# A one-core encoder step: mask products over 128 rows, and the last down set, final norm and output in an order written out by hand

## The chip, the cores and the metric

The kernel runs on one core of a Trainium2 chip. The metric is the device time of one execution in microseconds (us). Below, the engines have short names: PE is TensorE (matrix products; PEld its weight loads), DVE is VectorE, ACT is ScalarE, POOL is GpSimd, and SP is the engine that issues most transfers.

## What is computed

One layer of a streaming encoder, for 1024 prompt frames and 64 sample frames (1088 columns), with 1024 features. Two places matter here.

```python
s = einsum("bqhd,bkhd->bhqk", q, k) * SOFTMAX_SCALE
visible = (k_pos // CHUNK) <= (q_pos // CHUNK)        # CHUNK = 64 frames
s = where(visible, s, -1e30); p = softmax(s)
...
h = h + square(relu(rmsnorm(h, g_mlp) @ w_up)) @ w_down   # 1024 -> 4096 -> 1024
y = rmsnorm(h, g_final)       # h * rsqrt(mean(h*h) + 1e-6) * g_final
```

## The kernel before

**Attention.** For each of 8 heads and each of 8 blocks `i` of 128 queries, `scores` forms a score tile `S` in PSUM from three products (lines L1180 to L1182: every operand is split into a high and a low part), over 96 rows for even heads and 128 rows for odd ones. Only the last 128 columns of a tile need a mask, and it is added by one more product, L1184: `lhsT=mrow[:, 0:128], rhs=mrow[:, 128:256]`. `mrow` has one row: 128 zeros and ones, and 128 values that are 0 or -1e30; the product of the two halves is a 128x128 block that is -1e30 where a key isn't visible. There are 64 of these products. `negm` (DVE) takes the row maximum, ACT the exponential, PE transposes the result (`tr`, L1198), and PE multiplies with the values (`po`, L1208 to L1211). Up to three score tiles are in flight ahead of their transposes.

**The last down set.** The MLP's products are done by a scheme with 7 products in place of 8 on 2x2 blocks (`SEQ = "XYXYXZX"` names the PSUM tile of each of the 7; `TAKE` says which quarter `q[k][t]` of the output each is added to). A *set* `(g, jp)` is 7 products: `g` is one of 8 slices of the hidden features, `jp` one of two halves of the output features. The 1088 columns are two blocks `t` of 544 (`NH`), each in two halves `c` of 272 (`NC`). The last set (`g == 7, jp == 1`) does all 7 products for `c = 0`, then for `c = 1`, so that the final norm of the first columns can start early. Product `i` for one `c` is 12 matmuls of 272 columns (two feature blocks `jl`, two `k`, three high/low combinations), and is then added into `q` on DVE (`dn_evac`, L1809).

**Final norm and output.** `final_first` squares and sums the features that are final before the last set; `final_half(c, t)` squares the others on ACT, sums them (on PE, `col_sum`, into 68x4 columns), takes 1/sqrt by `rsqrt_col` (DVE, one ACT square root, DVE), spreads the result over 128 partitions by four transposes on PE (L1876), and multiplies: for `t = 1` ACT applies the gain and POOL the rows (L1885), for `t = 0` DVE does both in one instruction (L333), one bank of PSUM being read. 16 transfers of 272 KB write `y`, 14 issued by SP and 2 by ACT. All of this is written as generators that a `pump()` advances after each product, and a scheduler places each engine's instructions.

Of the kernel before, what the change touches and what calls it, by code (L numbers as in the profile page):

```python
# [22 lines left out]
EPS = 1e-6  # L23
# [6 lines left out]
def tile_hybrid_step(ctx: ExitStack, tc: tile.TileContext, I: dict, O: dict):  # L30
# [828 lines left out]
    mrow = phq.tile([1, 256], F32R, name="mrow")  # L859
    mraw = raw1([1, 256], "mraw")  # L860
# [953 lines left out]
    sqp, fin = [], []  # L1814

    def final_first():

        for c in range(2):
            cc = slice(NC * c, NC * c + NC)
            sqp.append(rq([128, 2, NC], f"fsq{c}"))  # L1820
            for t in range(2):
                s_ = rq([128, 2, 2, NC], f"fp{c}{t}")
                for k in range(2):
                    act.activation(s_[:, k], q4[k][t][:, 0:2, cc], AF.Square)
                e = dve if t else pool
                e.tensor_tensor(s_[:, 0], s_[:, 0], s_[:, 1], op=ALU.add)
                e.tensor_tensor(sqp[c][:, t], s_[:, 0, 0], s_[:, 0, 1], op=ALU.add)
                yield
        for k in range(2):
            for j in range(2):  # L1830
                z = q4[k][1][:, j]
                act.activation(z, z, AF.Copy, scale=g_fi[:, 4 * k + j:4 * k + j + 1])
            yield

    def final_half(c, t):

        cc = slice(NC * c, NC * c + NC)
        end = c == 1 and t == 0
        pr_ = fin[c][:, t]
        ps = pr_[:, NC:512]  # L1840
        sq = [wr4([128, 2, NC], f"fs{c}{t}{k}") for k in range(2)]
        ks = (0, 1)

        def col_sum(z, n):
            for j in range(4):
                pe.matmul(ps[:TT, 4 * n + j:4 * n + j + 1], lhsT=z[:, TT * j:TT * j + TT], rhs=ones, start=True, stop=True)

        if end:
            col_sum(sqp[c][:, t], 0)
        for k in ks:  # L1850
            for j in range(2):
                act.activation(sq[k][:, j], q4[k][t][:, 2 + j, cc], AF.Square)
                if end:
                    col_sum(sq[k][:, j], 1 + 2 * k + j)
            yield
        cl_ = [x[:TT, 4 * t:4 * t + 4] for x in col[:3]]
        tot = ps[:TT, 0:4]
        if end:
            tot = col[3][:TT, 0:4]
            dve.tensor_reduce(tot, ps[:TT, 0:20].rearrange("p (n j) -> p j n", j=4), axis=mybir.AxisListType.X, op=ALU.add)  # L1860
        else:
            e = dve if t else pool
            e.tensor_tensor(sq[0], sq[0], sq[1], op=ALU.add)
            e.tensor_tensor(sq[0][:, 0], sq[0][:, 0], sq[0][:, 1], op=ALU.add)
            e.tensor_tensor(sq[0][:, 0], sq[0][:, 0], sqp[c][:, t], op=ALU.add)
            yield
            col_sum(sq[0][:, 0], 0)
        rsqrt_col(cl_[0], tot, 1024, cl_[1:])
        if t:
            for k in range(2):  # L1870
                for j in range(2):
                    z = q4[k][t][:, 2 + j, cc]
                    act.activation(z, z, AF.Copy, scale=g_fi[:, 4 * k + 2 + j:4 * k + 3 + j])
        yield
        for j in range(4):
            pe.transpose(pr_[:, TT * j:TT * j + TT], cl_[0][:, j:j + 1].to_broadcast([TT, 128]), ident[:TT, :TT])  # L1876
        c0 = NH * t + NC * c
        if t:
            rows = rq([128, NC], f"f{c}{t}w")
            act.copy(rows, pr_[:, :NC])  # L1880
# [12 lines left out]
    for g in range(8):  # L1893
        for jp in range(2):
            last = g == 7 and jp == 1
            made = {}
            for cs in ([[0], [1]] if last else [[0, 1]]):
# [3 lines left out]
                for i, x in enumerate(SEQ):  # L1901
# [3 lines left out]
                    for jl in range(2):  # L1905
# [4 lines left out]
                        if last:  # L1910
                            o = o[:, jl:jl + 1]
# [138 lines left out]
```

## Time and profile before

| what | value |
|---|---|
| median of 3 runs | 1413.93 us (1413.08 to 1417.74) |
| the profiled execution's own time | 1413.71 us |
| its span, first to last instruction | 1411.6 us |
| mean granted TensorE clock, as a share of full speed | 0.973 |
| busy: PE / PEld / DVE / ACT / POOL | 94% / 90% / 75% / 47% / 48% of the span |

The profile is of one execution. The 2.1 us between its span and its own time lie outside of the instructions. PE is busy nearly throughout, so what counts is where PE's time goes, and what is left at the end when PE has no products any more.

### The profile page before, as it was taken

Reading aid. Unit: us, or ns where it says so; the run is one execution under the profiler, and the core shown is the slowest. Engines: PE = TensorE matmul, PEld = TensorE weight load, DVE = VectorE, ACT = ScalarE, POOL = GpSimd, SP = SyncE. Lnnn points to the kernel's source line nnn. Section 1 sums busy time; section 2 is a strip of 40 time slices with the busy share of each in tenths; the row PEclk is TensorE's granted clock in tenths of the full one; section 3 lists DMA queues with packets and bytes.
Section 4 is the critical chain, followed back from the end, with each engine's and each line's share of the span. In section 5 each row is a group of like instructions: output and inputs, shape, how many; then the busy total and the mean of one; then the engine's idle time right before and its main releaser. Section 6 shows DMA issues by size and latency. Waiting matters only on the chain.

```text
span 1411.6 us, 24894 instructions
## 1 busy us (share of the span) xinstructions
PE 1321.5 (94%) x9544; PEld 1264.7 (90%) x9544; DVE 1055.7 (75%) x1675; ACT 667.1 (47%) x1335; POOL 680.6 (48%) x642
## 2 busy tenths in 40 slices
PE   6999999989999996999789999999989999999994
PEld 6999988977887786999789999999979999999994
DVE  7679789775888767557895566565699788888766
ACT  6476577665777753223342332332446433334332
POOL 3656756151435426252465455455547446454543
PEclk9999999999999998999899999999999999999996
DMA  5111101210333234022224443443568345563103
GB/s 215 62 41 41 44 28 47 74 34 8 59 59 73 68 114 132 1 92 75 85 84 146 162 157 114 157 156 118 200 238 291 123 156 170 175 187 110 60 1 127
DMA packets 81145, 151.24 MB, mean 107 GB/s; under 512 B 10114, under 2 KB 28675, under 8 KB 81027
## 3 DMA queue, kind: packets, MB, share of 16 engines
q1 hardware_dynamic: 80482, 149.10, 32.9%
q8 instruction: 75, 1.23, 0.3%
q10 hardware_dynamic: 544, 0.56, 0.1%
q14 instruction: 44, 0.35, 0.1%
HBM read 98.53 MB, written 41.40 MB: 99 GB/s over the span
## 4 chain that ended last, share of the span: by engine, by line
PE 70%; DVE 14%; issue 4%; ACT 4%; DMA 3%; POOL 3%; SPq 0%; DVEq 0%; ACTq 0%; POOLq 0%
PE X L1653 3%; PE X L1654 3%; PE X L1652 3%; PE dX L1652 3%; PE dX L1654 3%; PE dX L1653 3%; PE pw L1473 2%; PE pw L1475 2%; PE tr L1198 2%; PE pw L1474 2%; POOL wl L51 2%; PE dY L1654 2%; DVE ho L51 2%; PE dY L1652 2%; PE Y L1652 2%
## 5 line engine op out<-in xcount | busy, mean ns | idle before, releaser
L51 POOL TENSOR_TENSOR wl<-ws,wl 128x512 fp32r<-128x512 f32 x101 | 161.1, 1596 | 235.6 <-ACT wl L1546 228.6
L51 POOL TENSOR_TENSOR wl<-wr,wl 128x512 fp32r<-128x512 f32 x135 | 209.7, 1562 | 106.3 <-ACT wl L1546 100.8
L1546 ACT CAST wl<-ws 128x512 fp32r<-128x512 f32 x102 | 63.4, 622 | 196.7 <-DVE ws L1534 95.5
L1652 PE MATMUL dX<-to,wl 128*128 128x272 f32 x496 | 144.0, 290 | 2.9 <-DVE q L1809 2.0
L1653 PE MATMUL dX<-to,wl 128*128 128x272 f32 x496 | 142.9, 288 | 0.7 <-DVE to L51 0.7
L1654 PE MATMUL dX<-to,wl 128*128 128x272 f32 x496 | 143.4, 290 | 0.0
L1652 PE MATMUL X<-ho,wl 128*128 128x272 f32 x448 | 128.0, 290 | 5.4 <-DVE rb L1671 3.8
L1653 PE MATMUL X<-ho,wl 128*128 128x272 f32 x448 | 128.8, 288 | 0.5 <-DVE ho L51 0.5
L1654 PE MATMUL X<-ho,wl 128*128 128x272 f32 x448 | 128.9, 289 | 0.0
L1546 ACT CAST wl<-wr 128x512 fp32r<-128x512 f32 x136 | 83.9, 621 | 89.3 <-PE dX L1654 34.7
L1809 DVE TENSOR_TENSOR q<-dX,q 128x544 f32<-128x544 f32 (+1 forms) x116 | 79.4, 697 | 29.1 <-PE dX L1654 28.9
L1532 DVE TENSOR_TENSOR ws<-wr,wr 128x512 f32<-128x512 f32 x34 | 28.1, 826 | 93.9 <-DMA wr<-in_w_up_dram 74.8
L1652 PEld LDWEIGHTS dX<-to,wl 128*128 128x128 f32 x496 | 93.4, 188 | 4.2 <-DVE q L1809 1.6
L1653 PEld LDWEIGHTS dX<-to,wl 128*128 128x128 f32 x496 | 94.0, 190 | 1.0 <-DVE to L51 1.0
L1654 PEld LDWEIGHTS dX<-to,wl 128*128 128x128 f32 x496 | 93.3, 188 | 0.0
L1652 PEld LDWEIGHTS X<-ho,wl 128*128 128x128 f32 x448 | 83.6, 188 | 6.7 <-DVE rb L1671 4.2
L1653 PEld LDWEIGHTS X<-ho,wl 128*128 128x128 f32 x448 | 84.4, 188 | 0.7 <-DVE ho L51 0.7
L51 DVE TENSOR_TENSOR to<-rr,to 128x1088 fp32r<-128x1088 f32 x56 | 84.1, 1506 | 1.0 <-ACT to L1727 1.0
L1654 PEld LDWEIGHTS X<-ho,wl 128*128 128x128 f32 x448 | 84.2, 188 | 0.0
L1652 PE MATMUL dY<-to,wl 128*128 128x272 f32 x256 | 74.5, 291 | 2.8 <-DVE rb L333 1.8
L1654 PE MATMUL dY<-to,wl 128*128 128x272 f32 x256 | 75.0, 293 | 1.6 <-POOL wl L51 1.6
L1653 PE MATMUL dY<-to,wl 128*128 128x272 f32 x256 | 74.0, 289 | 0.0
(685 smaller groups left out, 4706.5 us busy)
## 6 DMA issues: line engine op xcount, KB each, us to landing
rr<-rd SPq DMA_DIRECT2D x56, 544.0 KB, 5.0
wr<-in_w_up_dram SPq DMA_DIRECT2D x36, 512.0 KB, 4.4
wr<-in_w_dn_dram SPq DMA_DIRECT2D x32, 512.0 KB, 4.7
rd<-rc SPq DMA_DIRECT2D x16, 544.0 KB, 3.6
rd<-re SPq DMA_DIRECT2D x16, 544.0 KB, 3.5
rd<-ra SPq DMA_DIRECT2D x28, 272.0 KB, 2.6
xw<-in_x_dram SPq DMA_DIRECT2D x8, 544.0 KB, 7.3
hp<-in_x_dram SPq DMA_DIRECT2D x4, 1088.0 KB, 13.2
```

The lines of the kernel that those rows point to most:

```text
L51: eng.tensor_tensor(out, src, hi, op=ALU.subtract)
L1198: pe.transpose(tr[:, 128 * j:128 * j + 128], Pt[:, 128 * (j0 + j):128 * (j0 + j) + 128], ident)
L1473: pe.matmul(o, lhsT=w[kt][0][:, m_], rhs=rh, start=(kt == 0), stop=False)
L1474: pe.matmul(o, lhsT=w[kt][0][:, m_], rhs=rl, start=False, stop=False)
L1475: pe.matmul(o, lhsT=w[kt][1][:, m_], rhs=rh, start=False, stop=(kt == 3))
L1532: dve.tensor_tensor(s_, a21, a22, op=ALU.add)
L1546: act.copy(w[:, 0], src)
L1652: pe.matmul(o, lhsT=lh, rhs=rh, start=first, stop=False, skip_group_check=True)
L1653: pe.matmul(o, lhsT=lh, rhs=rl, start=False, stop=False, skip_group_check=True)
L1654: pe.matmul(o, lhsT=ll, rhs=rh, start=False, stop=last, skip_group_check=True)
L1809: dve.tensor_tensor(z, o[:, :, :NC], z, op=ALU.add)
```

## The change

`mrow` becomes 128 rows, the first as before and 127 of zeros, in the kernel and in the constant that is loaded. The mask product therefore runs over 128 rows; its result is the same.

The last set, the final norm and the output are taken out of the loop and of the generators and are written out in one list under `tc.manual_schedule()`, in which each engine keeps the order of the list. The small chain of the norm works on PSUM (`v`) where it worked on SBUF. For the last columns (`c = 1`) the rows are transposed twice, into the tile `dY` (`ps`) for DVE and into the tile `fin` for an ACT copy that POOL reads, so that both engines multiply. All early sums of squares go to POOL.

```diff
-    mrow = phq.tile([1, 256], F32R, name="mrow")
-    mraw = raw1([1, 256], "mraw")
+    mrow = phq.tile([128, 256], F32R, name="mrow")
+    mraw = raw1([128, 256], "mraw")
...
+    def norm_f(ps, t):
+
+        v, o = ps[:TT, t, NC:NC + 4], col[t][:TT, 0:4]
+        dve.tensor_scalar(v, v, 1.0 / 1024, EPS, op0=ALU.mult, op1=ALU.add)
+        act.activation(o, v, AF.Sqrt)
+        yield
+        dve.reciprocal(o, o)
+        dve.tensor_tensor(v, v, o, op=ALU.mult)
+        stt(v, v, -0.5, o, ALU.mult, ALU.mult)
+        stt(o, v, 1.5, o, ALU.add, ALU.mult)
+
+    def rows_f(ps, t):
+
+        for j in range(4):
+            pe.transpose(ps[:, t, TT * j:TT * j + TT], col[t][:TT, j:j + 1].to_broadcast([TT, 128]), ident[:TT, :TT])
...
+    with tc.manual_schedule():
+        early(0, 1)
+        products(0, 0)
+        take(0, 0)
+        early(0, 0)
+        products(1, 0)
+        take(1, 0)
+        for k in range(2):
+            gain_f(0, 1, k, 0)
+        products(2, 0)
+        take(2, 0)
+        early(1, 1)
+        products(3, 0)
+        take(3, 0)
+        square_f(0, 1, 0)
+        early(1, 0)
+        products(4, 0)
+        take(4, 0)
+        square_f(0, 1, 1)
+        for n in range(2):
+            add_f(0, 1, n)
+        for k in range(2):
+            gain_f(0, 1, k, 1)
+        products(5, 0)
+        take(5, 0)
+        square_f(0, 0, 0)
+        products(6, 0)
+        take(6, 0)
+        square_f(0, 0, 1)
+        products(0, 1, (0,))
+        fin = psa("fin")
+        col_sum(fin[:, 1, NC:], fs[0, 1, 0][:, 0])
+        n01 = norm_f(fin, 1)
+        next(n01)
+        add_f(0, 0, 0)
+        next(n01, None)
+        add_f(0, 0, 1)
+        products(0, 1, (1,))
+        take(0, 1)
+        gain_f(0, 0, 0, 0)
+        products(1, 1, (0,))
+        rows_f(fin, 1)
+        act.copy(rows[:, 0, 1], fin[:, 1, :NC])
+        for k, h in KH:
+            mul_pool(0, 1, k, h)
...
+        products(6, 1, (1,))
+        take(6, 1, slice(1, 2))
+        square_f(1, 0, 1, slice(1, 2))
+        rows_f(ps, 1)
+        mul_dve(ps, 1, 1, 0, 2)
+        sums = ps[:, 0, NC + 8:]
+        col_sum(sums, sqp[:, 1, 0])
+        for j in range(2):
+            col_sum(sums[:, 4 + 4 * j:], fs[1, 0, 1][:, j])
+        total(0, 3)
+        n10 = norm_f(ps, 0)
+        next(n10)
+        rows_f(fin, 1)
+        act.copy(rows[:, 1, 1], fin[:, 1, :NC])
+        for k in range(2):
+            mul_pool(1, 1, k, 0)
+        mul_dve(ps, 1, 1, 0, 3)
+        out_f(1, 1, 0, 1, 0)
+        next(n10, None)
+        rows_f(ps, 0)
+        rows_f(fin, 0)
+        for m in (2, 3):
+            mul_dve(ps, 1, 1, 1, m)
+        out_f(1, 1, 1, 1, 0)
+        act.copy(rows[:, 1, 0], fin[:, 0, :NC])
+        mul_pool(1, 0, 0, 0)
+        for k, h in KH[1:]:
+            for m in (2 * h, 2 * h + 1):
+                mul_dve(ps, 1, 0, k, m)
+            out_f(1, 0, k, h, h)
...
-    mrow = np.concatenate([low, (1 - low) * f4(-1e30)])[None]
+    mrow = np.zeros((128, 256), f4)
+    mrow[0] = np.concatenate([low, (1 - low) * f4(-1e30)])
```

In that list `products(i, c)` is the 12 matmuls of product `i` (6 for one `jl`), `take` their addition into `q` on DVE, `early` two squares on ACT and two sums on POOL, `square_f` a square on ACT, `gain_f` two gains on ACT, `add_f` sums of squares on DVE, `mul_pool` a product on POOL and its output transfer, `mul_dve` a product on DVE, and `total` the sum of the column sums.

What it moves on DVE in the middle of the last set, as the compiled order of the changed kernel has it (`dX`, `dY`, `dZ` are the product tiles of the first half of the columns, `q` the output quarters, `fs` squares, `fin` the norm's tile):

```order
L1859 TENSOR_TENSOR q_11266<-dX_14870,q_11266 128x2x272
L1882 TENSOR_TENSOR fs_14938<-fs_14938,fs_14958 128x544
L1884 TENSOR_TENSOR fs_14938<-fs_14938 128x272
L1885 TENSOR_TENSOR fs_14938<-fs_14938,sqp 128x272
L1859 TENSOR_TENSOR q_11263<-dZ_14967,q_11263 128x2x272
L1859 TENSOR_TENSOR q_11265<-dX_14870,q_11265 128x2x272
L1895 TENSOR_SCALAR fin<-fin 68x4
L1882 TENSOR_TENSOR fs_14981<-fs_14981,fs_14996 128x544
L1898 RECIPROCAL col_6965<-col_6965 68x4
```

The three sums L1882 to L1885 stand ahead of the last two additions of the first half (from `dZ` and `dX`), which were done as soon as their products were there before. On PE the column sums that need these DVE results stand six products into the second half (`dX_14998` is its first tile):

```order
L1653 MATMUL dX_14998<-to_0_14358,wl_17_0_14722 128x272
L1654 MATMUL dX_14998<-to_0_14358,wl_17_0_14722 128x272
L1890 MATMUL fin<-ones,fs_14938 68x1 x4
L1652 MATMUL dX_14998<-to_0_14358,wl_17_0_14722 128x272
L1653 MATMUL dX_14998<-to_0_14358,wl_17_0_14722 128x272
```

In the kernel before, PE met its first column sums of the final norm only near the end of the second half, with 18 of its products still to come. At the end of the program DVE had this order before (`fin` holds the rows of `c = 0`, `dY_15016` those of `c = 1`):

```order
L91 SCALAR_TENSOR_TENSOR col_6966<-col_6966,col_6965 68x4
L92 SCALAR_TENSOR_TENSOR col_6964<-col_6966,col_6964 68x4
L333 SCALAR_TENSOR_TENSOR q_11263<-q_11263,gains,fin 128x272 x4
L333 SCALAR_TENSOR_TENSOR q_11265<-q_11265,gains,fin 128x272 x4
L1860 TENSOR_REDUCE col_6967<-dY_15016 68x4
L84 TENSOR_SCALAR col_6965<-col_6967 68x4
L89 RECIPROCAL col_6964<-col_6964 68x4
L90 TENSOR_TENSOR col_6966<-col_6964 68x4
L91 SCALAR_TENSOR_TENSOR col_6966<-col_6966,col_6965 68x4
L92 SCALAR_TENSOR_TENSOR col_6964<-col_6966,col_6964 68x4
L333 SCALAR_TENSOR_TENSOR q_11263<-q_11263,gains,dY_15016 128x272 x4
L333 SCALAR_TENSOR_TENSOR q_11265<-q_11265,gains,dY_15016 128x272 x4
```

and it has this one now:

```order
L2002 TENSOR_REDUCE dY_15028<-dY_15028 68x4
L1895 TENSOR_SCALAR dY_15028<-dY_15028 68x4
L333 SCALAR_TENSOR_TENSOR q_11264<-q_11264,gains,dY_15028 128x272
L1898 RECIPROCAL col_6964<-col_6964 68x4
L1899 TENSOR_TENSOR dY_15028<-dY_15028,col_6964 68x4
L333 SCALAR_TENSOR_TENSOR dY_15028<-dY_15028,col_6964 68x4
L333 SCALAR_TENSOR_TENSOR col_6964<-dY_15028,col_6964 68x4
L333 SCALAR_TENSOR_TENSOR q_11266<-q_11266,gains,dY_15028 128x272 x2
L333 SCALAR_TENSOR_TENSOR q_11265<-q_11265,gains,dY_15028 128x272 x2
L333 SCALAR_TENSOR_TENSOR q_11263<-q_11263,gains,dY_15028 128x272 x2
L333 SCALAR_TENSOR_TENSOR q_11265<-q_11265,gains,dY_15028 128x272 x2
```

The eight products with `fin` are gone from DVE (POOL does those of `c = 0, t = 0` now), and eight follow the last small chain as before, of which two belong to `t = 1`. In the attention the order of every engine is unchanged.

## Rows read from the trace of the kernel before

**Rows 1.** Windows of the attention and of the end: busy by engine, clock, DMA.

```profile
334.00:507.00 173.00, 165.35 (x1014) 135.39 (x1014) 129.13 (x280) 124.54 (x285) 70.77 (x105) 0.99 0.27 54
...
1400.00:1412.00 12.00, 0.69 (x4) 0.51 (x4) 5.11 (x11) 0.00 (x0) 1.61 (x2) 0.50 0.78 256
```

**Rows 2.** Chain of waits in 334 to 507 us: shares by line.

```profile
by line: PE tr L1198 17.1%; PE S L1180 9.6%; PE po L1208 8.9%; PE S L1181 8.7%; PE po L1210 8.6%; PE S L1182 8.5%; PE S L1184 7.5%; ACT P L1190 3.6%; issue 3.2%; ACT yh L1264 2.2%; ACT PTh L1200 2.2%; PE pos L1021 2.0%; PE pv L811 2.0%; DMA
```

**Rows 3.** All instructions on mrow: ns min/median/max, first to last start, forms.

```profile
L1184 PE MATMUL S<-mrow x64: 321/322/471, 334.3 to 507.0; 1*128 1x128 f32 x64
L862 ACT CAST mrow<-mraw x1: 398/398/398, 291.1 to 291.1; 1x256 fp32r<-1x256 f32 x1
```

**Rows 4.** Timeline of PE, attention: start us, us, line, tiles, rows*columns of weights, form.

```profile
421.25 0.28 PE L1182 MATMUL S<-kT_h,qT_l 128*128 128x256 f32 x1
421.46 0.32 PE L1184 MATMUL S<-mrow 1*128 1x128 f32 x1
...
422.67 0.28 PE L1211 MATMUL po<-PTh,vh 128*128 128x256 f32 x1
422.78 0.23 PE L1180 MATMUL S<-kT_h,qT_h 96*128 96x128 f32 x1
422.85 0.28 PE L1181 MATMUL S<-kT_l,qT_h 96*128 96x128 f32 x1
422.96 0.28 PE L1182 MATMUL S<-kT_h,qT_l 96*128 96x128 f32 x1
423.16 0.32 PE L1184 MATMUL S<-mrow 1*128 1x128 f32 x1
423.41 0.38 PE L1208 MATMUL po<-PTh,vh 128*128 128x256 f32 x1
```

**Rows 5.** Timeline of PE, sample attention: one product over 64 rows, then 128.

```profile
342.90 0.38 PE L1021 MATMUL pos<-vn,PTsh 64*128 64x256 f32 x1
343.21 0.74 PE L1021 MATMUL pos<-vc,PTsl 128*128 128x256 f32 x4
```

**Rows 6.** Costliest groups, weight loads of the down products: busy, mean ns, idle before.

```profile
L1652 PEld LDWEIGHTS dX<-to,wl 128*128 128x128 f32 x496 | 93.4, 188 | 4.2 <-DVE q L1809 1.6
```

**Rows 7.** Timeline of PE, last set and end.

```profile
1364.28 0.29 PE L1652 MATMUL dX<-to,wl 128*128 128x272 f32 x1
...
1364.91 0.29 PE L1654 MATMUL dX<-to,wl 128*128 128x272 f32 x1
...
1388.10 1.09 PE L1846 MATMUL dY<-ones,fs 128*68 128x1 f32 x16
...
1401.96 0.69 PE L1876 MATMUL dY<-ident,col 68*128 68x68 f32 x4 [6.06 <-DVE col L92]
```

**Rows 8.** Timeline of DVE, last set and end.

```profile
1362.97 0.72 DVE L1809 TENSOR_TENSOR q<-dX,q 128x544 f32<-128x544 f32 x1 [0.79 <-PE dX L1654]
...
1390.50 0.16 DVE L90 TENSOR_TENSOR col<-col 68x4 f32<-68x4 f32 x1
...
1392.59 1.25 DVE L91 SCALAR_TENSOR_TENSOR col<-col,col 68x4 f32<-68x4 f32 x1
...
1395.06 3.34 DVE L333 SCALAR_TENSOR_TENSOR q<-q,gains,fin 128x272 f32<-128x272 f32 x8
...
1402.69 3.36 DVE L333 SCALAR_TENSOR_TENSOR q<-q,gains,dY 128x272 f32<-128x272 f32 x8 [0.87 <-PE dY L1876]
```

**Rows 9.** Timeline of POOL at the end.

```profile
1391.20 5.21 POOL L1885 TENSOR_TENSOR q<-q,f01w 128x544 f32<-128x544 f32 x4 [2.75 <-ACT f01w L1880]
```

**Rows 10.** Timeline of ACT in the last set.

```profile
1365.24 2.85 ACT L1824 ACTIVATE fp<-q 128x544 f32<-128x544 f32 x5
...
1378.15 0.92 ACT L1873 ACTIVATE q<-q,gains 128x272 f32<-128x272 f32 x2
```

**Rows 11.** Transfers, 1364 to 1412 us: rate in 40 slices of 1.2 us; last issues.

```profile
GB/s 0 0 0 0 0 0 0 0 0 0 0 14 0 0 0 0 0 0 0 0 0 0 0 7 159 73 0 205 354 366 356 359 332 191 323 330 325 330 17 0
...
1404.44 2.01 ACTq L1890 DMA_DIRECT2D out_y_dram<-q  x2
```

More of the change, by code (lines that the diff above doesn't have):

```diff
@@ L1812, in dn_evac @@
                 act.copy(z, o[:, :, :NC])
[L1814 to L1880, printed above, removed]
-        for k in range(2):
-            for h in range(2):
-                z = q4[k][t][:, 2 * h:2 * h + 2, cc]
-                if t:
-                    pool.tensor_tensor(z, z, rows[:, None, :].to_broadcast([128, 2, NC]), op=ALU.mult)
-                else:
-                    for j in range(2):
-                        n = 4 * k + 2 * h + j
-                        stt(z[:, j], z[:, j], g_fi[:, n:n + 1], pr_[:, :NC], ALU.mult, ALU.mult)
-                (nc.scalar if end and h else nc.sync).dma_start(O["y"][:, 4 * k + 2 * h:4 * k + 2 * h + 2, c0:c0 + NC], z)
-            yield
@@ new lines, in tile_hybrid_step @@
+            for i, x in enumerate(SEQ):
+                w = w_next()
+                while g == 0 and jp == 0 and len(Top[0]) < min(7, i + 2):
+                    next(tst)
+                for jl in range(2):
+                    first = (x, jl) not in made
+                    if first:
+                        made[x, jl] = psa(f"d{x}{g}{jp}{jl}")
+                    o = made[x, jl]
+                    for c in range(2):
+                        dn_product(w, o[:, c, :NC], g, i, jl, c, first)
+                    dn_evac(i, o, 2 * jp + jl, [0, 1])
+                if (jp == 0 and i >= 3) or (jp == 1 and i < 3):
+                    next(tst, None)
+                if 2 <= g < 6 and i == 3:
+                    residual((g - 2) // 2, (g - 2) % 2, jp)
+                pump()
@@ L1941, in tile_hybrid_step, with chunk, products @@
     while live:
         pump()
+    ws = [w_next() for _ in range(7)]
+    sqp = rq([128, 2, 2, NC], "sqp")
+    rows = rq([128, 2, 2, NC], "frows")
+    made = [{}, {}]
+    fs = {}
+    def chunk(k, t, c, m):
+        return q4[k][t][:, m, NC * c:NC * c + NC]
+    def products(i, c, jls=(0, 1)):
+        x = SEQ[i]
+        if x not in made[c]:
+            made[c][x] = psa(f"d{x}7{c}")
+        for jl in jls:
+            dn_product(ws[i], made[c][x][:, jl, :NC], 7, i, jl, c, i == SEQ.index(x))
```

134 lines of the change are left out of this document (89 added, 45 removed).

## The prediction

> **What bounds the kernel now.** I read the busy time by stretch first, then the chain of waits in the two stretches that the change touches, then the timeline of the engine that the chain runs over. In the attention PE is busy 165.35 of 173 us, while DVE and ACT are busy 129 and 125 [rows 1]: whatever PE saves there can come off the time. The chain there runs mostly over PE lines, and the mask product L1184 holds 7.5% of it, 13.0 us [rows 2], though it is only 64 products of 128 columns [rows 3]. The timeline shows why. Behind a product of 256 columns the mask starts 0.21 us later (421.25 to 421.46), behind one of 128 columns 0.20 us later (422.96 to 423.16), and the product behind the mask starts 0.25 us after it (423.16 to 423.41). Without a mask between them such products follow each other at 0.11 us (422.67 to 422.78, 422.85 to 422.96) [rows 4]. So PE pays on entering a product over fewer rows and again on leaving it. A product over 64 rows shows the same on leaving: 0.31 us to the next (342.90 to 343.21) [rows 5]. Going from 128 to 96 rows costs nothing (422.67 to 422.78).
>
> At the end PE is not the bound. In the last 12 us it is busy 0.69, DVE 5.11, and the transfers hold 0.78 of the DMA engines [rows 1]. PE goes from the products to column sums at 1388.1 [rows 7], and DVE finishes its last output product at 1402.69 + 3.36 = 1406.05 [rows 8]. Between lie two small chains on DVE, with eight products of the first columns (3.34 us) in between. A link of such a chain takes 0.16 us alone (1390.50), and 1.25 us (1392.59) [rows 8] while POOL is at work [rows 9]: it waits for POOL's instruction in hand. The products with an operand in PSUM do not: eight in 3.34 us under the same POOL work.
>
> **The mask products.** Now a mask takes 0.20 + 0.25 = 0.45 us from the start of the product ahead to the start of the next (0.46 behind 256 columns). Over 128 rows no change of rows is left behind 128-row scores, nor, by the step 422.67 to 422.78, behind 96-row ones; two steps of 0.11 make 0.22 [rows 4]. That is 0.24 us each, 15.4 us for 64. Of the chain's 13.0 us at 0.25 each, 52 of the 64 lie on it [rows 2], so 12.5 us. I take off 1 us for waits that open when PE gets through sooner, and have **-11.5 us**. Bounds: 15.4 us if every mask counts; 8 us if the time that PE idles there now (173 - 165.35 = 7.65 us, [rows 1]) grows by half. Everything behind the attention starts earlier by the same amount, and its weight loads are issued in the order of that work, so I give nothing back there.
>
> Here a page speaks against the change. The Trainium skill, "TensorE: Matmul & The Clock Gate", section "Why this matters for your kernels", says that a single product over 32 rows takes the same time as one over 128. By that rule alone the mask saves nothing. The Trainium skill, "TensorEngine Tiling (Array Packing)", section "Key Properties", says that changing the tiling mode drains the engine, and the steps of rows 4 and 5 agree with this one; the first rule then holds for a product among its like only.
>
> The larger constant (128 rows, not 1) costs nothing: its cast ends 43 us before the first mask (291.1, 334.3) [rows 3] and takes 398 ns for any number of rows. If that cover were gone it would cost those 0.4 us and the load of 128 KB, under 1 us by the output's rate [rows 11].
>
> **The last set, in the time of the profile before.** (1) Its first product starts at 1364.28, and five steps later it is 1364.91: 0.126 us a step [rows 7]. The first half, 84 products, ends at 1374.9 unhindered: additions take 0.72 us [rows 8] against 1.51 us for the product between.
>
> (2) Six products on, at 1375.6, PE reaches the column sums in `fin`, which by the new order need three sums and two additions on DVE first, and those sums need ACT's second square. ACT, from 1365.2: three squares and four gains are over by 1369; the square of product 3's sum can't start before 1370.3 + 0.2 + 0.72 = 1371.3, and then come four squares at 0.57 [rows 10]: 1373.7. The sums, 0.65 + 0.35 + 0.35 us, work on SBUF alone, and POOL is then in the last of its eight early sums, so I add 1.5 us for waits on POOL (each is at most one POOL instruction, 5.21/4 = 1.30 us [rows 9]): 1376.7. Two additions: 1378.2. **PE waits 2.6 us** (1.1 without POOL). Queued behind on PE are all other products; this is what the fixed order adds.
>
> (3) Then 78 products (9.8 us), 28 column sums (at 1.09/16 = 0.07 us [rows 7], 1.9 us), eight transposes (0.69 us for four at half the clock [rows 7]; I take 0.45 at the full one, 0.9 us), and waits of 1.9 us: 0.5 for the first rows (behind a square root and four small links), 1.1 for the second (ACT has eight gains at 0.46 [rows 10] ahead of the root), 0.3 for the last squares of `t = 1`. The last product ends at 1392.7, 4.6 us later than before.
>
> (4) The last column sums need two sums of squares from POOL, which has eight products at 1.30 ahead, from 1381.6: 1393.6. Twelve column sums at half the clock end at 1395.4. The last small chain, seven links at 0.2 us (PSUM operands: no wait on POOL) and one product of 0.42 between them, ends at 1397.1; the transposes 0.8; eight products 3.3 us [rows 8]. DVE ends at **1401.2, against 1406.05**. The gain is that the eight products of the first columns went to POOL, and that 1.25 us links are gone.
>
> (5) Output. Before, six transfers fell to the last 2.5 us of issuing, and the program ended 5.55 us after DVE's last product, the transfers running at some 330 GB/s [rows 11]. Now seven of 272 KB (0.84 us each) are issued from 1399.1 on, 5.9 us of transfer in place of 5.1: I give 0.85 us back. The end comes at **-4.0 us**. Bounds: -7 (no waits on POOL in step 2, outputs no denser than before); +5.8 (a rival below).
>
> Sum: 1413.71 - 11.5 - 4.0 = **1398.2 us**; the profiled execution is 0.2 us under the median of the runs.
>
> **Rivals.** A: the other engines eat the mask's gain. DVE works 129 of what would be 160 us [rows 1], in short dependent steps; if only 4 us come through, 1405.7. Against it: the chain holds little but PE [rows 2]. Chance 0.10.
>
> B: the mask's price is not its rows but its place (a fresh weight load, the end of a group), so 128 rows change nothing: 1413.7 - 4.0 = 1409.7. Against it: the 64-row step [rows 5]. By the rule of the Trainium skill, "TensorE: Matmul & The Clock Gate", section "Why this matters for your kernels", it would be so. Chance 0.06.
>
> C: the wait of step 2 lets PE's clock fall from 2.4 to 1.2 GHz. The last rows have 0.50 for the clock [rows 1], after a stretch of small sums and waits. If it stays there for the 78 products, +9.8 us: 1413.7 - 11.5 + 5.8 = 1408.0. For one short fall, part of it hides in the later waits. Chance 0.07.
>
> D, on the other side: a mask over all rows no longer has its weight load beside other work, nor has the product behind it. Two loads of 0.188 us [rows 6] on top of 0.22 make 0.60, 0.14 more than now: 64 x 0.14 = +9.0, and 1413.7 + 9.0 - 4.0 = 1418.7. It turns the result slower from 0.13 us per mask on. Against it: loads of 128 rows of 0.188 us lie beside products that start every 0.126 us. Chance 0.03.
>
> **How the numbers follow.** My forecast has 0.74. Its own range, from a mask term of 8 to 15.4 and an end of -1 to -7 with neither extreme in both at once, is 1392 to 1403. With A that makes 1391.5 to 1406, and B, C and D (0.16) stay out in the main. A measurement of this kernel tells 0.3% (4.2 us) from no change; faster by more are the forecast, A and C, 0.91; within it B, 0.06; slower D, 0.03.
>
> **What would show it.** In the attention: 128 rows on L1184, steps of 0.11 us on both sides of it, its share of the chain well under 5%, and the whole from 334 to 507 some 11.5 us shorter; PE's busy share there should not rise. A stretch that is shorter by under 5 us means A, unchanged steps B. In the last set: a wait of PE of 1 to 3 us at the first column sums, on DVE; smaller ones at the rows; the small links at 0.2 us; DVE's last product some 5 us nearer to the set's first product than before (41.8 us); the last 5.5 us transfers alone. I would be wrong above all if the clock falls in the set, or if POOL's queue (eight products, then the two sums) ends later than I take it and holds the last column sums.

## The result, and the profile after

| | before | changed |
|---|---|---|
| median, 4 runs each | 1415.84 us (1413.08 to 1422.04) | 1399.51 us (1394.58 to 1401.94) |
| ratio | | 0.9874, 95% interval 0.9829 to 0.9919 |
| profiled execution, its span, its clock | 1413.71, 1411.6, 0.973 | 1398.26, 1396.4, 0.976 |

Faster by 1.26%; the forecast was 1398.2. But only a part of the time came from where the forecast had it. The busy time by stretch of the changed kernel (the attention, the MLP up to the last set, the last set's products, the rest). Behind each stretch stand its length, the busy time and number of instructions of PE, PEld, DVE, ACT and POOL, the granted clock of TensorE as a share of full speed, and the load of the transfers, as in [rows 1]:

```profile
334.00:495.50 161.50, 150.40 (x1017) 135.15 (x1016) 125.99 (x281) 122.67 (x286) 69.85 (x105) 0.97 0.29 58
495.50:1349.70 854.20, 809.79 (x6274) 800.51 (x6273) 624.50 (x782) 308.19 (x486) 421.83 (x275) 0.98 0.41 137
1349.70:1379.60 29.90, 27.10 (x233) 26.16 (x233) 16.85 (x39) 18.63 (x43) 20.09 (x17) 0.95 0.21 75
1379.60:1396.40 16.80, 5.28 (x42) 4.70 (x40) 5.70 (x17) 1.29 (x4) 3.92 (x3) 0.50 0.41 134
```

The attention takes 161.5 us in place of 173.0 [rows 1], **-11.5**. That is the mask term to the decimal, but with a clock of 0.97 in place of 0.99: in part a coincidence (see the section on why the prediction was right). The last set starts 14.6 us earlier (1364.28 to 1349.65), so **-3.1** came between, where the program is unchanged. The traces of the kernels below with a mask of 96 or 128 rows take 852.9 to 858.7 us for that same stretch, from the last mask to the last set (before 857.3), so 3.1 us lie within what it varies from one execution to the next; what varies was not isolated. From the last set's first product to the end are 46.8 us against 47.3 before: **-0.6**, where -4.0 had been forecast.

All instructions on `mrow`, as in [rows 3]:

```profile
L1184 PE MATMUL S<-mrow x64: 221/226/376, 334.5 to 495.5; 128*128 128x128 f32 x64
L862 ACT CAST mrow<-mraw x1: 408/408/408, 291.5 to 291.5; 128x256 fp32r<-128x256 f32 x1
```

The chain of waits in the attention (334 to 496 us), as in [rows 2]:

```profile
by line: PE tr L1198 11.1%; PE S L1180 9.5%; ACT P L1190 9.0%; PE S L1181 7.9%; PE S L1182 7.7%; PE po L1208 7.3%; PE po L1210 6.5%; ACT PTh L1200 5.3%; issue 4.3%; DVE negm L1187 4.0%; DMA wgr<-in_w_glu_dram 3.6%; DVE PTl L51 2.7%; ACT yh 
```

The mask product is no longer among the parts that the answer shows, and the share of ACT's exponential (L1190) rose from 3.6% to 9.0%: some of what PE saves, it now waits for others.

The cast of the larger constant took 408 ns where 398 was forecast. PE's timeline at two masks, behind 256 and 512 columns, answers to [rows 4]; below them, from 1360.80 on, stands the last set, to be held against [rows 7]:

```profile
414.11 0.28 PE L1182 MATMUL S<-kT_h,qT_l 128*128 128x256 f32 x1
414.22 0.22 PE L1184 MATMUL S<-mrow 128*128 128x128 f32 x1
414.28 0.62 PE L1198 MATMUL tr<-ident,P 128*128 128x128 f32 x4
...
421.51 0.39 PE L1182 MATMUL S<-kT_h,qT_l 96*128 96x512 f32 x1
421.74 0.23 PE L1184 MATMUL S<-mrow 128*128 128x128 f32 x1
421.80 0.39 PE L1198 MATMUL tr<-ident,P 128*128 128x128 f32 x2
...
1360.80 0.29 PE L1654 MATMUL dX<-to,wl 128*128 128x272 f32 x1
1362.01 0.62 PE L1890 MATMUL fin<-ones,fs 128*68 128x1 f32 x8 [0.93 <-DVE fs L1885]
...
1365.37 0.45 PE L1906 MATMUL fin<-ident,col 68*128 68x68 f32 x4 [1.14 <-DVE col L333]
...
1369.64 0.45 PE L1906 MATMUL fin<-ident,col 68*128 68x68 f32 x4 [0.20 <-DVE col L333]
...
1372.99 0.60 PE L1890 MATMUL dY<-ones,sqp 128*68 128x1 f32 x8
1373.45 1.12 PE L1890 MATMUL dY<-ones,fs 128*68 128x1 f32 x16
1374.44 0.37 PE L1652 MATMUL dZ<-to,wl 128*128 128x272 f32 x1
...
1375.28 1.09 PE L1890 MATMUL dY<-ones,fs 128*68 128x1 f32 x16
1376.23 0.37 PE L1652 MATMUL dX<-to,wl 128*128 128x272 f32 x1
1376.44 0.29 PE L1653 MATMUL dX<-to,wl 128*128 128x272 f32 x1
1376.57 0.34 PE L1654 MATMUL dX<-to,wl 128*128 128x272 f32 x1
1376.70 0.43 PE L1652 MATMUL dX<-to,wl 128*128 128x272 f32 x1
1376.93 0.43 PE L1653 MATMUL dX<-to,wl 128*128 128x272 f32 x1
...
1379.42 0.43 PE L1654 MATMUL dX<-to,wl 128*128 128x272 f32 x1
1379.65 0.66 PE L1906 MATMUL dY<-ident,col 68*128 68x68 f32 x4
1380.99 1.04 PE L1890 MATMUL dY<-ones,sqp 128*68 128x1 f32 x8 [0.68 <-DVE q L333]
1381.88 1.95 PE L1890 MATMUL dY<-ones,fs 128*68 128x1 f32 x16
```

Behind 256 columns the mask now starts 0.11 us later (before 0.21), and what follows 0.06 us after it (before 0.25). In the last set three things are to be seen. The steps of the products go from 0.13 us (1376.57 to 1376.70) to 0.23 (1376.70 to 1376.93): TensorE's clock falls from 2.4 to 1.2 GHz at 1376.7, with nine of the set's products and the last column sums still to come; before, the clock was 1.00 over the products (1364.30 to 1388.10) and fell behind them. One `col_sum` is four products in the program, but stands in the trace as eight records, and takes 0.46 us to the next (1372.99 to 1373.45). And the last column sums wait 0.68 us for a DVE product.

DVE in the last set and at the end, as in [rows 8]:

```profile
1358.95 1.44 DVE L1882 TENSOR_TENSOR fs<-fs,fs 128x544 f32<-128x544 f32 x1 [0.86 <-ACT fs L1872]
...
1361.42 0.44 DVE L1885 TENSOR_TENSOR fs<-fs,sqp 128x272 f32<-128x272 f32 x1
1361.78 0.72 DVE L1859 TENSOR_TENSOR q<-dZ,q 128x544 f32<-128x544 f32 x1
...
1363.91 0.73 DVE L1882 TENSOR_TENSOR fs<-fs,fs 128x544 f32<-128x544 f32 x1 [0.71 <-ACT fs L1872]
...
1380.34 0.50 DVE L333 SCALAR_TENSOR_TENSOR q<-q,gains,dY 128x272 f32<-128x272 f32 x1
1383.87 0.17 DVE L2002 TENSOR_REDUCE dY<-dY 68x4 f32<-68x12 f32 x1 [3.03 <-PE dY L1890]
...
1385.56 0.16 DVE L333 SCALAR_TENSOR_TENSOR col<-dY,col 68x4 f32<-68x4 f32 x1
1386.52 3.36 DVE L333 SCALAR_TENSOR_TENSOR q<-q,gains,dY 128x272 f32<-128x272 f32 x8 [0.81 <-PE dY L1906]
```

The small links take 0.17 us with POOL at work, as forecast. DVE's last product ends at 1386.52 + 3.36 = 1389.88, 40.2 us after the set's first product (before 41.8, forecast 36.9); the program ends 6.5 us later (before 5.55). And between 1380.84 and 1383.87 DVE has nothing to do.

### The profile page after: what moved, and what is told of

Its sections match the earlier page's. It is cut to its first block, busy times and chain, and to the rows that moved or that the text cites. A ratio compares the mean times of both kernels' runs of the same rounds, so it can differ in the third digit from the quotient of the medians.

```text
span 1396.4 us, 24944 instructions
## 1 busy us (share of the span) xinstructions
PE 1305.7 (94%) x9568; PEld 1262.2 (90%) x9568; DVE 1038.9 (74%) x1655; ACT 668.5 (48%) x1342; POOL 682.5 (49%) x648
## 4 chain that ended last, share of the span: by engine, by line
PE 71%; DVE 14%; ACT 5%; issue 4%; DMA 3%; POOL 2%; SPq 0%; DVEq 0%; ACTq 0%; POOLq 0%
PE dX L1652 4%; PE dX L1654 4%; PE dX L1653 4%; PE X L1653 3%; PE X L1654 3%; PE X L1652 3%; PE pw L1473 2%; PE pw L1475 2%; PE pw L1474 2%; PE dY L1654 2%; PE dY L1652 2%; DVE ho L51 2%; PE dY L1653 2%; PE pq L207 2%; PE pq L208 2%
## 5 line engine op out<-in xcount | busy, mean ns | idle before, releaser
L51 POOL TENSOR_TENSOR wl<-ws,wl 128x512 fp32r<-128x512 f32 x101 | 161.5, 1600 | 237.4 <-ACT wl L1546 232.8
L1652 PE MATMUL dX<-to,wl 128*128 128x272 f32 x512 | 149.2, 292 | 2.6 <-DVE q L1809 1.4
L1654 PE MATMUL dX<-to,wl 128*128 128x272 f32 x512 | 148.3, 290 | 0.0
L1653 PE MATMUL dX<-to,wl 128*128 128x272 f32 x512 | 147.7, 289 | 0.0
L1652 PEld LDWEIGHTS dX<-to,wl 128*128 128x128 f32 x512 | 96.8, 189 | 4.4 <-issue 1.2
L1653 PEld LDWEIGHTS dX<-to,wl 128*128 128x128 f32 x512 | 97.4, 190 | 0.0
L1654 PEld LDWEIGHTS dX<-to,wl 128*128 128x128 f32 x512 | 97.0, 190 | 0.0
L1809 DVE TENSOR_TENSOR q<-dX,q 128x544 f32<-128x544 f32 x108 | 75.9, 717 | 25.6 <-PE dX L1654 25.6
```

The source lines that it names most:

```text
L51: eng.tensor_tensor(out, src, hi, op=ALU.subtract)
L1652: pe.matmul(o, lhsT=lh, rhs=rh, start=first, stop=False, skip_group_check=True)
L1653: pe.matmul(o, lhsT=lh, rhs=rl, start=False, stop=False, skip_group_check=True)
L1654: pe.matmul(o, lhsT=ll, rhs=rh, start=False, stop=last, skip_group_check=True)
L1809: dve.tensor_tensor(z, o[:, :, :NC], z, op=ALU.add)
```

## The experiments

The first four kernels divide the change. The times of the kernel before beside them: 1417.23 us, median of 23 runs (1412.84 to 1427.92).

**The mask alone.** The kernel before with only the edits on `mrow`:

```diff
-    mrow = phq.tile([1, 256], F32R, name="mrow")
-    mraw = raw1([1, 256], "mraw")
+    mrow = phq.tile([128, 256], F32R, name="mrow")
+    mraw = raw1([128, 256], "mraw")
...
-    mrow = np.concatenate([low, (1 - low) * f4(-1e30)])[None]
+    mrow = np.zeros((128, 256), f4)
+    mrow[0] = np.concatenate([low, (1 - low) * f4(-1e30)])
```

> The kernel before with the mask product over 128 rows and nothing else; same result. Theory M (leaving the 128-row weights for a 1-row product and coming back costs PE 0.24 us per mask): the last mask of the attention starts 11 to 13 us earlier than in before (507.0 us there), the mask's steps are 0.11 us on both sides, and the whole time falls by 11 to 15 us (-0.8 to -1.05%), the last 3 us of it by chance of the clock. Rival B (the price lies in the mask's place, not in its rows): attention and whole time unchanged, 0 +- 4 us. Rival A (the other engines eat it): -4 us. The last set should look as in before: 41.8 us from its first product to DVE's last product.

Measured: 1403.93 us (6 runs), ratio 0.9889 (0.9860 to 0.9917). Last mask at 495.2 us, then 857.8 us to the last set, then 47.3 us to the end, as before. The mask's own line in that trace:

```profile
L1184 PE MATMUL S<-mrow x64: 221/226/415, 334.5 to 495.2; 128*128 128x128 f32 x64
```

Theory M holds; A and B fall, and with them D of the prediction, since the steps around a mask got shorter, not longer.

**The end alone.** The changed kernel with `mrow` of one row:

```diff
-    mrow = phq.tile([128, 256], F32R, name="mrow")
-    mraw = raw1([128, 256], "mraw")
+    mrow = phq.tile([1, 256], F32R, name="mrow")
+    mraw = raw1([1, 256], "mraw")
...
-    mrow = np.zeros((128, 256), f4)
+    mrow = np.zeros((1, 256), f4)
```

> The changed kernel with a mask product over 1 row again: the end is changed alone; same result. By the prediction's end term: -4.0 us against before, DVE's last product some 37 us after the set's first product. By the pair of traces in hand: only -0.6 us (+- 3 us for the chance of the clock elsewhere), DVE's last product 40 to 40.5 us after the set's first product, and TensorE's clock falling to half within the set, ahead of its last products. A clock that stays at full until the products are over would give -2 to -3 us and make the fall in the trace in hand a chance of that one execution.

Measured: 1417.66 us (12 runs), ratio 0.9992 (0.9966 to 1.0019): no change that the runs can tell. The interval reaches to -0.34%, 4.8 us, so the times alone do not rule out the -4.0 either. Yet the trace of this execution has an end that is 3 us shorter than before's:

```profile
336.00:519.30 183.30, 176.96 (x1019) 145.87 (x1017) 130.13 (x282) 125.38 (x286) 70.86 (x105) 0.92 0.25 51
...
1377.20:1406.20 29.00, 26.20 (x235) 25.35 (x234) 16.84 (x39) 18.28 (x43) 20.07 (x17) 1.00 0.22 77
1406.20:1421.50 15.30, 3.44 (x42) 2.98 (x39) 5.62 (x17) 1.60 (x5) 3.92 (x3) 0.62 0.45 147
```

The granted clock is 1.00 through the set's products. DVE's last product comes 37.8 us after the first, the end 44.4 (before 47.3). So the new order has run with and without a fall of the clock inside the set, and the fall cost 2.4 us (46.8 against 44.4). (The attention of this execution has 0.92 for the clock and is 10 us longer than before's, which is why its time is high as a whole.)

**The mask over 64 and over 96 rows.** The same three lines, 64 rows in the one and 96 in the other:

```diff
-    mrow = phq.tile([128, 256], F32R, name="mrow")
+    mrow = phq.tile([64, 256], F32R, name="mrow")
```

> The changed kernel with the mask product over 64 rows (the first as before, 63 of zeros); same result. Theory M1 (what costs is a change between products over few rows and products over many, and 64 rows are on the few side, as the one 64-row product of the sample attention shows on leaving, 0.31 us): the mask costs what 1 row cost, steps of 0.20 and 0.25 us, last mask 11 to 12 us later than in the changed kernel, time +11 to +15 us. Theory M2 (what costs grows with the rows that differ): half of it, +6 us. Rival B: 0.

> The changed kernel with the mask product over 96 rows; same result. Theory M1: 96 rows count as 128 (scores over 96 rows behind products over 128 follow at 0.11 us): no change, 0 +- 4 us, last mask at 495.5 +- 1.5 us. Theory M2 (it grows with the rows that differ): a quarter of the loss, +3 us.

Measured with 64 rows: 1416.94 us (10 runs), ratio 0.9990 (0.9964 to 1.0015), the whole gain lost. PE's timeline at a mask, and the set's window:

```profile
423.01 0.39 PE L1182 MATMUL S<-kT_h,qT_l 128*128 128x512 f32 x1
423.33 0.32 PE L1184 MATMUL S<-mrow 64*128 64x128 f32 x1
423.58 1.09 PE L1198 MATMUL tr<-ident,P 128*128 128x128 f32 x8
```

```profile
1371.80:1400.80 29.00, 26.20 (x235) 25.36 (x234) 16.84 (x39) 18.30 (x43) 20.06 (x17) 1.00 0.22 77
```

Behind 512 columns the mask starts 0.32 us later and what follows 0.25 us after it, where over 128 rows these are 0.23 and 0.06. With 96 rows: 1399.43 us (4 runs), ratio 0.9858 (0.9819 to 0.9898), last mask at 495.2 us. So 64 rows cost what one row costs, and 96 what 128 cost: M1 holds, M2 falls.

These four kernels show one thing more. With 96 rows the mask costs what it does with 128, and the end is the new one; the mask alone has the old end. Their times are 1399.43 us (1397.82 to 1400.71) and 1403.93 (1401.98 to 1406.60): on top of the wide mask the new end goes with 4.5 us less, on top of the mask of one row with nothing (1417.66 against 1417.23). Why the two changes do not simply add up was not found. In the pair of traces 3.8 of the 4.4 us lie between the last mask and the last set (854.1 against 857.8 us), not in the end.

**The end, four edits.** The runs of the kernel before beside them: 1418.2 us (7 runs, 1409.92 to 1425.72). A few runs can't tell 1 to 2 us here, so these are read from the traces.

Column sums of `t = 1` moved apart:

```diff
-        products(4, 1)
+        products(4, 1, (0,))
+        col_sum(sums, sqp[:, 1, 1])
+        products(4, 1, (1,))
...
         products(5, 1, (0,))
-        col_sum(sums, sqp[:, 1, 1])
-        for j in range(2):
-            col_sum(sums[:, 4 + 4 * j:], fs[1, 1, 0][:, j])
+        col_sum(sums[:, 4:], fs[1, 1, 0][:, 0])
         products(5, 1, (1,))
+        col_sum(sums[:, 8:], fs[1, 1, 0][:, 1])
```

> The changed kernel with two of the five column sums of t = 1 (last columns) moved ahead on PE, between products 4 and 5 and between the halves of 5, where they stood together. Theory S (the stretch of 20 column-sum products, with little work in them for PE, is what lets its clock fall to half 27 us after the set's first product): the clock stays at full until the products are over, DVE's last product comes 37.5 to 38.5 us after the set's first in place of 40.2, the whole falls by 2 to 2.5 us. Rival W (the waits at the first rows, further ahead, are what counts) or rival T (it depends on when the set starts): fall at 27 us as now, 40.2 us, no change.

Measured: 1399.78 us. The clock does not fall at 27 us, but for a short while at 17.8 us after the set's first product; DVE's last product at 39.3 us. What S forecast, a clock at full until the products are over, did not come: the loss moved, it did not go. But the edit is no full test of S. Three of the five column sums still stand in one piece, now behind product 5:

```profile
1378.61 1.58 PE L1890 MATMUL dY<-ones,fs 128*68 128x1 f32 x24
```

And this execution's set started 2.3 us later than the changed kernel's, so it does not tell whether the moved sums or the later start took away the fall at 27 us.

The first column sums later:

```diff
-        products(0, 1, (0,))
+        products(0, 1)
         fin = psa("fin")
         col_sum(fin[:, 1, NC:], fs[0, 1, 0][:, 0])
...
-        products(0, 1, (1,))
         take(0, 1)
```

> The changed kernel with the first column sums in fin put six products later on PE (behind the whole first product of the last columns, not its first half). If the wait of step 2 costs what it takes in the trace (0.93 us): that wait is gone, DVE gets product 0 while the sums run, and the set's last product starts 0.7 to 0.9 us earlier, POOL's first product by rows 0 to 0.8 us later. Rival: the wait moves to the first rows (1.14 us there now, 1.9 then) and nothing is won, since the chain behind the column sums starts no sooner. By the prediction's step 2 (2.6 us) more would be won. Time: -0.8 or 0 us, under what a few runs tell, so read from the trace.

Measured: 1400.82 us. PE at the two places:

```profile
1361.90 0.62 PE L1890 MATMUL fin<-ones,fs 128*68 128x1 f32 x8 [0.19 <-DVE fs L1885]
...
1365.26 0.45 PE L1906 MATMUL fin<-ident,col 68*128 68x68 f32 x4 [1.80 <-DVE col L333]
```

The wait of 0.93 is 0.19 now, and that of 1.14 is 1.80: it moved, as the rival has it. What sets POOL's first product is the chain on DVE and ACT (16.7 us after the set's first product in both kernels). Here the clock fell at 16.9 us, behind that longer wait, was back at 23.7, and DVE's last product comes at 40.8.

The set later:

```diff
+        products(0, 0)
         products(0, 0)
         take(0, 0)
```

> The changed kernel with the 12 products of the last set's product 0 for the first columns done twice (the first time for nothing), so that all behind it comes 1.5 us later with the same distances. Rival T (whether the clock falls in the set depends on when the set falls in the program, since the same end begun 14.6 us or more later kept its clock until 32.7 us after its first product, behind the products): the clock falls elsewhere than at 27 us after the (second) first product; if behind the products, DVE's last product comes 37.8 us after it, and the whole is 1 us shorter in spite of the 1.5 us more work. Theory S or W (the work around it decides alone): fall at 27 us again, 40.2 us, the whole 1.5 us longer.

Measured: 1399.74 us, no slower than the changed kernel although 1.5 us of work is added.

```profile
1353.70:1382.80 29.10, 26.32 (x236) 25.47 (x235) 16.12 (x38) 17.20 (x42) 19.54 (x17) 1.00 0.21 72
```

Clock 1.00 in the set; DVE's last product 37.8 us after the second first product, the end 44.4: the numbers of the end that was tried alone. What T forecast came: the same work, with the same distances, kept the clock here and lost it in the changed kernel. But where it falls in the program does not decide it alone. The next kernel, whose PE work in the set is the changed kernel's, started its set at 1354.4 us, between this one's (1353.7) and one further below (1354.6) that both kept the clock, and lost it at 26.5 us.

The last sums in another tile (`total` reads them there):

```diff
-        sums = ps[:, 0, NC + 8:]
+        sums = fin[:, 0, NC + 8:]
         col_sum(sums, sqp[:, 1, 0])
```

> The changed kernel with the last 12 column sums written into the tile fin in place of dY, out of which DVE reads its product by rows at that time. Theory H (PE's wait of 0.68 us there, ended by DVE's product on dY, is for the tile, though other columns of it are read and written): the wait is gone, DVE's last product comes 0.5 to 0.7 us earlier, 39.6 us after the set's first. Rival: PE waits there for POOL's sums of squares, the operand, as the prediction's step 4 has it: no change. Time: -0.6 or 0, read from the trace.

Measured: 1401.12 us. PE at that place:

```profile
1384.79 0.66 PE L1906 MATMUL dY<-ident,col 68*128 68x68 f32 x4
1385.24 1.00 PE L1890 MATMUL fin<-ones,sqp 128*68 128x1 f32 x8
```

The column sums follow the transposes at 0.45 us, without a wait, where it was 1.34. From the set's last product to DVE's last are 9.5 us in place of 10.5. Theory H holds: the wait was for the tile, which DVE was reading in its other half, not for POOL's sums, which are over at 1378.4 in the changed kernel. Whether the chip asks for this wait or only the program's own semaphores do, no run shows. But the outputs give half of it back: 7.0 us from DVE's last product to the end in place of 6.5.

**The last four.** (Kernel before beside them: 1418.19 us, 11 runs.)

The work of `t = 1` drawn ahead:

```diff
         rows_f(ps, 1)
-        mul_dve(ps, 1, 1, 0, 2)
-        sums = ps[:, 0, NC + 8:]
+        rows_f(fin, 1)
+        for k in range(2):
+            for m in (2, 3):
+                mul_dve(ps, 1, 1, k, m)
+            out_f(1, 1, k, 1, 0)
+        act.copy(rows[:, 1, 1], fin[:, 1, :NC])
+        for k in range(2):
+            mul_pool(1, 1, k, 0)
+        sums = made[1]["Z"][:, 0, NC + 8:]
         col_sum(sums, sqp[:, 1, 0])
...
         next(n10)
-        rows_f(fin, 1)
...
```

> The changed kernel with the work of the block t = 1 (last columns) drawn ahead at the end: its rows go into fin right behind those into dY, its four DVE products and its two POOL products stand ahead of the last column sums, which are written into the product tile dZ (free by then), so that PE does not wait for DVE there; six DVE products are left behind the last small chain in place of eight and two of them. Theory (in the gap of 3 us that DVE has ahead of the last column sums, and of 6 us that POOL has, this work is free, and four of the eight last transfers leave 2 to 3 us sooner): from the set's last product to DVE's last 8.6 to 9.2 us in place of 10.5 at half clock (7.3 to 7.7 in place of 9.0 at full), from there to the end 5.2 to 5.8 in place of 6.5, the whole -2.5 us. Rival (POOL's products, now beside DVE's chain, hold its small links as in the kernel before, 1.25 us instead of 0.17): DVE's last product no earlier or up to 2 us later, the whole -1 to +2.

Measured: 1397.04 us (6 runs), ratio 0.9842 (0.9808 to 0.9876). DVE at the end, and the two last windows:

```profile
1384.07 1.71 DVE L333 SCALAR_TENSOR_TENSOR q<-q,gains,dY 128x272 f32<-128x272 f32 x4
1385.89 0.17 DVE L2003 TENSOR_REDUCE dY<-dZ 68x4 f32<-68x12 f32 x1
...
1387.11 0.16 DVE L333 SCALAR_TENSOR_TENSOR col<-dY,col 68x4 f32<-68x4 f32 x1
1388.08 2.54 DVE L333 SCALAR_TENSOR_TENSOR q<-q,gains,dY 128x272 f32<-128x272 f32 x6 [0.81 <-PE dY L1906]
```

```profile
1354.60:1383.60 29.00, 26.18 (x235) 25.34 (x235) 16.84 (x39) 18.33 (x43) 20.06 (x17) 1.00 0.22 77
1383.60:1395.80 12.20, 3.15 (x41) 2.86 (x39) 5.61 (x17) 1.55 (x5) 3.95 (x3) 0.62 0.56 185
```

The four products of `t = 1` lie in DVE's gap, the links stay at 0.17 us beside POOL. With the clock at 1.00 in the set, as in the delayed one, from the last product to DVE's last are 7.2 us in place of 9.0, and from there to the end 5.2 in place of 6.5: 3.1 us less (41.2 against 44.4 from the set's first product to the end). By the medians it is 2.5 us less than the changed kernel. The rival falls.

The waits filled, and the sums apart as above:

```diff
         products(0, 1, (0,))
+        products(0, 1, (0,))
         fin = psa("fin")
...
         products(1, 1, (0,))
+        products(1, 1, (0,))
         rows_f(fin, 1)
```

> The changed kernel with six products repeated ahead of the first column sums in fin and six ahead of the first rows (work for nothing, in waits of 0.93 and 1.14 us), and the column sums of t = 1 spread as in the run that moved them. Theory W + S (idle time and small sums in the set together are what lets the clock fall in it, wherever the set lies): the clock stays at full until the products are over, DVE's last product 37.6 to 38.4 us after the set's first, the whole -2 us. Rival T alone (chance of place): a fall inside the set again, 39 to 40.5 us, no change.

Measured: 1400.99 us (4 runs). The waits of PE were 0.17 and 0.38 us, and yet the clock fell 28.4 us after the set's first product, and DVE's last product came at 40.3. What W + S forecast did not come. It shows that the waits are not needed for a fall; S it does not rule out, since here too three column sums stand in one piece, 25.5 to 27.0 us after the set's first product.

Both of these in one kernel (the diffs of the two together):

> Both of the last two: waits filled and column sums spread, and the work of t = 1 drawn ahead at the end. If both theories hold: DVE's last product 36 to 36.7 us after the set's first, 5.2 to 5.8 us to the end, the whole 4 to 5 us under the changed kernel (about 1395), 1.5% under the kernel before. If only the drawing ahead holds: -2.5 us; if neither: 0 to +1.

Measured: **1395.21 us** (6 runs, 1393.12 to 1398.34), ratio 0.9832 (0.9795 to 0.9869), the fastest of all. DVE at the end:

```profile
1385.55 2.54 DVE L333 SCALAR_TENSOR_TENSOR q<-q,gains,dY 128x272 f32<-128x272 f32 x6 [0.55 <-PE dY L1906]
```

DVE's last product ends 36.2 us after the set's first, 5.2 us before the end, and the clock is at full in the set. This is what the drawing ahead gives (36.1 and 5.2); the intervals of the two overlap, and whether the filling adds anything can't be told. Up to the last column sums PE's work in the set is that of the kernel just before, which started its set 0.2 us earlier and lost the clock.

Two outputs left out of the changed kernel:

```diff
         mul_dve(ps, 1, 1, 0, 3)
-        out_f(1, 1, 0, 1, 0)
...
             mul_dve(ps, 1, 1, 1, m)
-        out_f(1, 1, 1, 1, 0)
```

> The changed kernel without two of its last eight output transfers (the second feature pairs of t = 1 in the last columns, 0.27 MB each, are left out, so that this part of the output is missing). Theory O (the transfers of the end run at the rate of the channel, some 330 GB/s, so their number sets the 6.5 us from DVE's last product to the end): 4.8 to 5.2 us. Rival L (it is what the last transfer alone needs): 6.2 to 6.5 us.

Measured (one execution, a span of 1398.1 us):

```profile
1389.33 3.35 DVE L333 SCALAR_TENSOR_TENSOR q<-q,gains,dY 128x272 f32<-128x272 f32 x8 [0.81 <-PE dY L1906]
```

From DVE's last product to the end are 5.45 us in place of 6.54. Two transfers make 1.1 us, between what O (1.3 to 1.7) and L (0 to 0.3) say. The run that drew them ahead took 5.2 us with all of them, four issued 2.2 us and more before the other four. Together this speaks for their crowding at the end as what costs the difference; what makes up the other 5 us was not tried.

## Why the prediction was right, and where it was wrong

The set in each profiled execution, in us after the set's first product (the set's start is the time in its execution; the set's last product starts 28.8 to 31.5 us after the first with the new end, 23.7 with the old):

| kernel | set starts | clock falls | DVE's last product | the end |
|---|---|---|---|---|
| changed | 1349.65 | 27.0 | 40.2 | 46.8 |
| mask of 96 rows | 1349.3 | 27.2 | 40.1 | 46.7 |
| end alone | 1377.2 | 32.7 | 37.8 | 44.4 |
| mask of 64 rows | 1371.8 | 32.6 | 37.8 | 44.3 |
| set delayed (from the second first product) | 1353.7 | 33.0 | 37.8 | 44.4 |
| work of `t = 1` ahead | 1354.6 | 32.0 | 36.1 | 41.2 |
| sums moved apart | 1352.0 | 17.8 to 21.2, then 34.9 | 39.3 | 45.8 |
| first sums later | 1349.5 | 16.9 to 23.7, then 34.0 | 40.8 | 47.3 |
| sums in another tile | 1354.4 | 26.5 | 39.8 | 46.8 |
| waits filled | 1351.7 | 28.4 | 40.3 | 46.8 |
| waits filled, work ahead | 1351.9 | 33.5 | 36.2 | 41.4 |
| two outputs less | 1351.3 | 17.9 to 21.3, then 28.2 | 41.3 | 46.8 |
| old end (before; mask alone) | 1364.3; 1353.05 | 25.8; 26.5 (behind the products) | 41.8; 41.5 | 47.3; 47.3 |

**The mask term was right** in cause: it alone makes most of the result (a ratio of 0.9889, where both changes give 0.9874), and 64 rows take it back whole. That its size came out to the decimal (-11.5 of -11.5) is luck, for two reasons. The first is its parts. The step into the mask went as forecast, 0.21 to 0.11 us behind 256 columns, but the step out of it went to 0.06 us at 47 of the 64 masks, not to 0.11. So a mask saves 0.29 us at most places, where I had 0.24. PE's busy time in the attention fell by 15.0 us (165.35 to 150.40), and its idle time there rose from 7.65 to 11.1: 3.5 us opened as waits where I took off 1. The two errors cancel. The second is the clock. The attention had 0.99 before and 0.97 in the changed kernel, which by these two means is some 3 us of the changed kernel's time (an estimate). The other two traces with a mask of 1 or 64 rows take 182.5 and 178.9 us from the first mask to the last, at 0.92 and 0.94, where the kernel before takes 172.7; the eleven with 96 or 128 rows take 158.8 to 161.1, at 0.97 or 0.98. So the pair in hand shows about the least that the wide mask gives. Whether products over few rows also bring the clock down was not tried.

Rival B falls, and with it the rule that it rests on. The Trainium skill, "TensorE: Matmul & The Clock Gate", section "Why this matters for your kernels", says that a single product over 32 rows takes the same time as one over 128. Among products over 96 and 128 rows the traces differ from it: a product over 1 or 64 rows costs 0.24 to 0.29 us more (32 rows were not run). The Trainium skill, "TensorEngine Tiling (Array Packing)", section "Key Properties", says that changing the tiling mode drains the engine; the steps into and out of the 64-row mask, 0.32 and 0.25 us against 0.23 and 0.06 with 128 rows, agree.

**The end term was mis-sized**: -4.0 forecast, -0.6 in the profiled execution, -3.0 where the clock holds. (By the times it is worth 0 to 4.5 us, as said above, so these two are sizes of single executions.) By its steps:

- Step 2: the wait at the first column sums was 0.93 us, not 2.6. The sums on DVE did wait for POOL, as forecast (1.44 us for one of 0.73), and were over 12.2 us after the set's first product (12.4 forecast). But the two additions, 1.5 us of the forecast wait, were not waited for; the column sums need only L1885, and DVE did the additions while PE summed.
- Step 3: column sums were under-sized by nearly half. I read the 16 records of [rows 7] as 16 products; they are 8. The 28 products are 56 records at 0.058 us, 3.3 us, not 1.9. The waits at the rows were 1.14 and 0.20 us where I had 0.5 and 1.1. The longer sums and the shorter wait of step 2 nearly cancel: the last product started 28.8 us after the first where the clock held, 29.8 where it fell (its end was forecast for 28.4).
- Step 4: the holder of the last column sums was not POOL, whose two sums end at 1378.4 (28.8 us after the set's first product, 29.3 forecast), but DVE's product on the same tile, 0.68 to 0.79 us. That was missing, and the twelve column sums were 24 records: 2.7 us at half the clock, where 1.8 had been allowed (1.5 where the clock held).
- Step 5: the outputs gave back 1.0 us (0.85 forecast).
- Rival C came true in part, in another place than it said: the clock fell not at the wait of step 2 but 27 us into the set, soon after the column sums of `t = 1` (2.4 of the 3.2 us from 1372.99 to 1376.23), and for 9 products, not 78. It cost 2.4 us, the table's 46.8 against 44.4.

**The rest had no term.** 3.1 us came off between the attention and the last set, where the program is unchanged. The same stretch took 852.9 us in one of these kernels and 858.7 in another, so the forecast could not have it; that it came the right way is luck. Without it the two traces would differ by 12.1 us and the time would be 1401.6, inside the range.

What lets the clock fall at one place of the set rather than another stays open. Waits and column sums lie ahead of the falls, but filling the waits did not keep the clock up, in one execution, and the sums were never taken fully apart. The work alone does not decide it, since the delayed set and the set with the work ahead kept the clock and the changed kernel's lost it. Nor does the set's start alone: sets begun at 1353.7 and 1354.6 us kept the clock, one begun at 1354.4 lost it. So all sizes here that hang on the clock are those of the execution that was traced. That the mask alone gives -13.3 us by the medians where its trace pair gives -11 fits with the quick attention of the profiled execution before; that execution lies 3.5 us under the median of the 23 runs.

## What to carry to other kernels

A product over few rows (1 and 64 here) among products over 96 or 128 costs PE 0.24 to 0.29 us here, with 128 columns; pad its operands with zeros, and subtract what PE then waits for the other engines. At a program's end, ask for each engine what lies in its gaps: drawing work and outputs ahead into a gap of 3 us was worth as much (3.1 us) as the whole hand-written order (3.0), in traces where the clock held. Before a sum counts on a row with xN, count how many instructions of the program stand behind that N. And before a size is read from one trace, look at the same stretch in other executions: unchanged code differed here by 5.8 us.

## What was not expected of the hardware

- 96 rows cost as much as 128, 64 as much as 1 (steps behind 512 columns 0.32 and 0.25 us against 0.23 and 0.06).
- A float32 product of one column appears as two records of 0.058 us each at the full clock, 0.11 at half.
- PE's write to one half of a PSUM tile waited 0.68 us for DVE's read of the other half, and not when written to another tile (whether the chip or only the program's own semaphores ask for it, no run shows).
- The same 30 us of PE work lost its clock in one execution and kept it in another: 46.8 against 44.4 us to the end.
